# The mixer of a state-space and Fourier diffusion step: order of issue rebuilt per pair (zeros behind the additions, decay factors two pairs ahead, transposes, tables and state matrices one pair later)

## The chip, the core and the metric

The kernel runs on one core of a Trainium2 chip. TensorE multiplies matrices, VectorE and GpSimd do elementwise work, ScalarE does functions and copies, SyncE issues most DMAs. Every engine works through its own queue in order and waits for the others by semaphores. The metric is device time in microseconds of one execution.

## What is computed

Two token sequences (1024 noisy latent tokens, 128 context tokens; 1024 channels) pass two layers. Layer 0 mixes tokens by an S5 state-space recurrence, layer 1 by a Fourier transform; behind each mixer stands a gated ConvFFN, and adaLN columns modulate all of it. Only the S5 mixer is touched here:

```python
abar = jnp.exp(lam * dt)
bbar = ((abar - 1.0) / lam)[..., None] * bmat
bu = jnp.einsum('blgc,gpc->blgp', u, bbar)
bu = bu.at[:, edge].add(abar * h0)
_, h = lax.associative_scan(_linear_recurrence, (a, bu), axis=1, reverse=reverse)
y = jnp.real(jnp.einsum('gcp,blgp->blgc', cmat, h))
```

There are 64 groups of 16 channels with 64 complex states each, in two directions; both sequences go through one pass.

## The kernel before

The mixer takes tokens in frames of eight: KW = 146 columns are 128 frames of the long sequence, two separating columns, and 16 of the short one. What happens inside a frame is a matrix (T, "kernel matrix"); what goes from frame to frame is a scan with the decay of eight steps, in coordinates turned by a phase, so that the scan is real. Groups are worked on in pairs per lane half: a block b is eight groups, four pairs (pr = 0 to 3), and the loop in `run` goes over i = 4b + pr = 0 to 31. All is in float32.

For a pair i:

- `vmm(i)`: TensorE multiplies the frames u by the transposed matrices PT into a PSUM tile V (two buffers), L1503. For i = 2 to 6 it also does a part of the adaLN columns in the same tile (`ada_mm`), finished later by `ada_end`.
- `vin(i)`: ScalarE writes decay factors `dec` (two instructions, L1524) and the columns between the four parts of V (zeros, L1527); VectorE turns V by the phase: B = V sn (L1532), V = V cs (L1533), two additions (L1534, L1535); ScalarE takes the final states (Fin, L1537) and writes one zero column and the initial states h0 (L1538, L1539).
- `scan(i)`: VectorE scans V in place (L1543).
- `vout(i)`: VectorE turns back, into C1 and C2 (L1554 to L1556).
- `wmm(i)`: TensorE adds T times u (L1566) and CA times C (L1572) in one PSUM tile y; ScalarE copies it to `ysb` (L1578).

For a block: `make_p` makes the products P (L1412, L1417, on GpSimd from block 2 on, one buffer) and transposes them on TensorE (`tr[0]`, `tr[1]`: L1425, copied to PT by ScalarE, L1428). `tables` makes cosine and sine: s0 and s1 on VectorE (s0: L1308, L1309; s1: L983, L984), Abs on ScalarE (L1314), four sines and four cosines there (L1322). `make_ca` makes the matrices CA in five GpSimd steps (L1365 to L1370), their `ends` on ScalarE (L1374, L1375), and b-bar (`bb`, L1383 to L1394). `make_t` multiplies Bb by CA (L1447, 64 matmuls in two banks "misc", which the transposes and `make_u` use too), copies the result to kc (L1457 to L1459, ScalarE), adds on GpSimd, and SyncE stores kc to DRAM and loads it back as T. `make_u` normalizes the input of a later block on TensorE and ScalarE (L1475, L1479); `load_u`, `load_x`, `loads` and `store_y` are DMAs on SyncE.

The order of issue is written out by hand: what the loop issues first stands first in each engine's queue. In an iteration come vmm(i + 1), scan(i), vin(i + 1), vout(i), wmm(i - 1), ada_end, and then the block's work for that pr. `pl` is a list of functions called at the end, `late` one called behind it. An instruction on a tile waits for earlier writes of that tile by another engine, as B here waits for the zeros, whose columns it does not read.

Of the kernel before, what the change touches and what calls it, by code (L numbers as in the profile page):

```python
# [16 lines left out]
D = 1024  # L17
# [947 lines left out]
class Ssm:  # L965
# [231 lines left out]
    def squares(self):  # L1197
# [18 lines left out]
        tiles.append(self.sg.tile([128, 1, D], F32, tag="P", bufs=1, name="xt"))  # L1216
# [180 lines left out]
    def make_p(self, b):  # L1397
# [10 lines left out]
        def prod(h, i):  # L1408
            def f():
                if not qs:  # L1410
                    qs.append(self.sg.tile([128, 8, 8], F32, tag="gs", bufs=1, name="gs"))
                    E.tensor_tensor(qs[0], self.G[:, 0, gs], self.G[:, 1, gs], OP.add)  # L1412
                if i == 0:
                    Ps[h] = self.sg.tile([128, 3, 4, 8, 16], F32, tag="P", bufs=1, name="P")
                g = (qs[0], self.G[:, 1, gs], self.G[:, 0, gs])[i]
                hs = slice(4 * h, 4 * h + 4)
                E.tensor_tensor(Ps[h][:, i], g[:, hs, :, None].to_broadcast([128, 4, 8, 16]), x[i][:, hs], OP.mult)  # L1417
            return f
# [96 lines left out]
    def vin(self, i):  # L1515
# [5 lines left out]
        dec = self.sp.tile([128, 2, 2, 148], F32, tag="dec", bufs=2, name="dec")  # L1521
        self.dec[i] = dec
        for dr in range(2):
            nc.scalar.activation(dec[:, :, dr], self.mask[:, None, dr].to_broadcast([128, 2, 148]), AF.Copy,  # L1524
                                 scale=self.r8[:, 2 * i + dr:2 * i + dr + 1])
        f = V.rearrange("p g k -> p (g k)")
        nc.scalar.activation(f[:, V0 + 147:V0 + 147 + 592].rearrange("p (s k) -> p s k", k=148)[:, :, 0:2],  # L1527
                             self.zero[:, None, :].to_broadcast([128, 4, 2]), AF.Copy)
# [9 lines left out]
        nc.scalar.activation(zf[:, :, 130], self.zero, AF.Copy)  # L1538
        nc.scalar.activation(zf[:, :, 0:167:166], self.h0[:, :, 2 * i:2 * i + 2], AF.Copy)  # L1539

# [51 lines left out]
    def run(self):  # L1592
# [47 lines left out]
        call(ca1[1:2])  # L1640
        self.vin(0)
# [6 lines left out]
        nv = 2  # L1648
        for i in range(n + 1):
            b, pr = divmod(i, 4)  # L1650
            n1, n2 = b + 1 < 8, b + 2 < 8
            if nv < n and nv <= i + 1:
                self.vmm(nv)
                nv += 1
# [4 lines left out]
            if i < n:  # L1659
                self.vout(i)  # L1660
            if i:
                self.wmm(i - 1)
# [8 lines left out]
            pl = []  # L1671
            late = [lambda: self.n.early(i - 27)] if i >= 27 else []
            if pr == 0:
# [4 lines left out]
                if n1:  # L1678
                    pp, tr = self.make_p(b + 1)
                    if b:  # L1680
                        tb = self.tables(b + 1)
                        call(tb[:2])
                    call(pp[0])
                    late = tr[0] + tb[2:3]
                if n2 and b:
                    ca, ends, bb = self.make_ca(b + 2)
                    pl = ca[:1] + [lambda: bb[0](self.nc.gpsimd)]
                if not b:
                    pl = ca1[2:] + [ends1]
                    second = Later(self.nc.vector)  # L1690
                    self.phases(second, rest)
                    self.phases16(second, rest)
                    late += [lambda: self.powers(rest, [second])]
            if pr == 1:
                if n1:
                    call(pp[1])
                    late = tb[3:]
                if not b:
                    ca, ends, bb = self.make_ca(2)
                if n2:  # L1700
                    pl = ca[b > 0:3]
                    if b + 3 < 8:
                        self.loads(b + 3)
            if pr == 2:
                if n1:
                    late = tr[1] + [lambda: self.make_t(b + 1)()]
                if n2:
# [3 lines left out]
                    pl = ca[3:4]  # L1711
            if i == 7:
                late = [self.last_frame]
            if pr == 3 and n2:
                self.make_u(b + 2)
                pl = ca[4:] + [ends]
                if b + 3 < 8:
                    self.load_x(b + 3)
            call(pl)
# [157 lines left out]
```

## Time and profile before

| | us |
|---|---|
| median of 3 runs (2499.51 to 2502.55) | 2499.62 |
| profiled execution, its own time | 2499.67 |
| its span, first to last instruction | 2497.9 |
| mixer loop, from the second B (L1532) to the last vout | 70.8 to 381 |
| TensorE busy, share of the span | 93% |
| mean granted TensorE clock | 0.97 |

The loop is an eighth of the run; behind it the kernel is a long row of matmuls, in which TensorE is busy nearly all the time. A timeline row gives start, duration, engine, line and tiles; the brackets tell how long the engine had been idle and which instruction ended that. A granted clock of 1 is TensorE's full speed, 2.4 GHz; 0.5 is 1.2 GHz.

### The profile page before, as it was taken

Reading aid. Unit: us, or ns where it says so; the run is one execution under the profiler, and the core shown is the slowest. Engines: PE = TensorE matmul, PEld = TensorE weight load, DVE = VectorE, ACT = ScalarE, POOL = GpSimd, SP = SyncE. Lnnn points to the kernel's source line nnn. Section 1 sums busy time; section 2 is a strip of 40 time slices with the busy share of each in tenths; the row PEclk is TensorE's granted clock in tenths of the full one; section 3 lists DMA queues with packets and bytes.
Section 4 is the critical chain, followed back from the end, with each engine's and each line's share of the span. In section 5 each row is a group of like instructions: output and inputs, shape, how many; then the busy total and the mean of one; then the engine's idle time right before and its main releaser. Section 6 shows DMA issues by size and latency. Waiting matters only on the chain.

```text
span 2497.9 us, 35759 instructions
## 1 busy us (share of the span) xinstructions
PE 2311.4 (93%) x14754; PEld 2228.0 (89%) x14754; DVE 1499.9 (60%) x2407; ACT 868.4 (35%) x1320; POOL 697.0 (28%) x462
## 2 busy tenths in 40 slices
PE   4668679999999999999999999999999999999996
PEld 3567569787999999999999999989999999999996
DVE  7766766889656454564455473965554555545556
ACT  4444445223523322223222444442232222332234
POOL 6355410226222211222112242622221112211124
PEclk8788799999999999999999999999999999999998
DMA  6323239666111111111111212111111111110112
GB/s 210 101 65 75 59 92 322 220 211 211 35 43 51 44 41 34 35 51 51 35 34 43 68 43 72 60 39 46 44 51 36 33 43 43 51 43 31 38 43 76
DMA packets 94522, 182.33 MB, mean 73 GB/s; under 512 B 16948, under 2 KB 57204, under 8 KB 93336
## 3 DMA queue, kind: packets, MB, share of 16 engines
q1 hardware_dynamic: 90824, 170.67, 21.7%
q0 software_dynamic: 2096, 6.62, 0.8%
q8 instruction: 117, 1.92, 0.3%
q10 hardware_dynamic: 1440, 2.75, 0.3%
q14 instruction: 45, 0.37, 0.0%
HBM read 163.70 MB, written 11.53 MB: 70 GB/s over the span
## 4 chain that ended last, share of the span: by engine, by line
PE 72%; DVE 17%; issue 4%; ACT 3%; DMA 1%; POOL 1%; DVEq 0%; ACTq 0%; POOLq 0%
PE acc L199 62%; DVE c L308 3%; DVE dl L602 2%; DVE dh L602 2%; PE f L839 2%; PE misc L1447 2%; DVE X L916 1%; PE y L1572 1%; DMA w_ada<-w_ada 1%; DVE h L222 1%; PE V L1503 1%; PE f L749 1%; DVE X L363 1%; DVE X L364 1%; PE misc L1425 1%
## 5 line engine op out<-in xcount | busy, mean ns | idle before, releaser
L199 PE MATMUL acc<-h,uh 128*128 128x384 f32 (+1 forms) x4992 | 1015.3, 338 | 1.9 <-DVE d L910 1.3
L199 PEld LDWEIGHTS acc<-h,uh 128*128 128x128 f32 x4992 | 885.2, 188 | 17.7 <-issue 13.2
L183 POOL TENSOR_TENSOR ul<-raw,uh 128x1024 fp32r<-128x1024 f32 x104 | 283.2, 2723 | 1242.2 <-ACT uh L182 1242.2
L199 PE MATMUL acc<-h,ul 128*128 128x384 f32 (+1 forms) x2496 | 571.2, 337 | 0.0
L308 DVE SCALAR_TENSOR_TENSOR c<-t,cw,c 128x896 f32<-128x896 f32 x704 | 347.3, 563 | 202.3 <-ACT c L305 202.3
L199 PEld LDWEIGHTS acc<-h,ul 128*128 128x128 f32 x2496 | 448.2, 189 | 0.0
L182 ACT ACTIVATE uh<-raw 128x1024 fp32r<-128x1024 f32 x108 | 113.6, 1052 | 547.0 <-PE acc L199 501.8
L300 DVE COPY wb<-acc 128x2 f32<-128x2 f32 x88 | 14.0, 159 | 406.1 <-PE acc L199 406.1
L363 DVE SCALAR_TENSOR_TENSOR X<-acc,MOD,X 128x768 f32<-128x768 f32 x168 | 170.1, 1012 | 118.3 <-PE acc L199 118.3
L199 PE MATMUL acc<-gh,dh 128*128 128x384 f32 x960 | 220.8, 337 | 18.4 <-DVE X L365 18.4
L199 PE MATMUL acc<-gl,dh 128*128 128x384 f32 x960 | 218.4, 335 | 0.0
L199 PE MATMUL acc<-gh,dl 128*128 128x384 f32 x960 | 218.2, 334 | 0.0
L199 PEld LDWEIGHTS acc<-gh,dh 128*128 128x128 f32 x960 | 168.8, 188 | 27.1 <-PE acc L199 23.6
L199 PEld LDWEIGHTS acc<-gh,dl 128*128 128x128 f32 x960 | 171.3, 188 | 0.0
L199 PEld LDWEIGHTS acc<-gl,dh 128*128 128x128 f32 x960 | 171.3, 188 | 0.0
L336 ACT ACTIVATE gh<-c 128x1152 fp32r<-128x1152 f32 x44 | 51.4, 1169 | 329.2 <-DVE c L331 290.9
L303 ACT ACTIVATE t<-t,wb 128x1024 f32<-128x1024 f32 x88 | 101.4, 1153 | 152.8 <-DVE t L301 152.8
L183 POOL TENSOR_TENSOR dl<-raw,dh 128x1024 fp32r<-128x1024 f32 x40 | 99.8, 2515 | 165.3 <-ACT dh L182 165.3
L305 ACT ACTIVATE c<-t,cb,cw 128x1152 f32<-128x1152 f32 x88 | 118.9, 1351 | 2.9
L301 DVE TENSOR_TENSOR t<-acc,R 128x1152 f32<-128x1152 f32 x88 | 118.6, 1348 | 0.0
L326 ACT ACTIVATE c<-c 128x1152 f32<-128x1152 f32 x44 | 51.4, 1167 | 152.4 <-DVE c L308 152.3
L1503 PE MATMUL V<-u,PT 128*64 128x146 f32 x512 | 45.7, 328 | 62.0 <-DVE C L1556 61.9
(327 smaller groups left out, 2677.6 us busy)
## 6 DMA issues: line engine op xcount, KB each, us to landing
raw<-w_up SPq DMA_DIRECT2D x88, 512.0 KB, 3.6
w_ada<-w_ada SPq DMA_DIRECT2D x80, 512.0 KB, 5.1
raw<-w_down SPq DMA_DIRECT2D x44, 512.0 KB, 3.6
w_ada<-w_ada SPq DMA_DIRECT2D x8, 1024.0 KB, 5.6
raw<-w_glu SPq DMA_DIRECT2D x16, 512.0 KB, 4.7
u<-hb SPq DMA_DIRECT2D x64, 73.0 KB, 3.3
y_scratch<-ysb SPq DMA_DIRECT2D x8, 584.0 KB, 3.5
xt<-x SPq DMA_DIRECT2D x9, 512.0 KB, 8.8
```

The costliest lines, as they stand in the source:

```text
L182: nc.scalar.activation(hi, raw, AF.Copy)
L183: (E or nc.gpsimd).tensor_tensor(lo, raw, hi.bitcast(F32), OP.subtract)
L199: mm(outs[j], lhsT=w, rhs=r[j], start=first and i == 0, stop=last and i == 2)
L301: nc.vector.tensor_tensor(t.rearrange("p (a b) -> p a b", a=3), p[:, :, :384], self.R.rearrange("p (a b) -> p a b", a=3), OP.mult)
L303: nc.scalar.activation(t[:, :NS], t[:, :NS], AF.Identity, bias=wb[:, 0:1])
L305: nc.scalar.activation(c, t, AF.Identity, bias=cb[:, ui:ui + 1], scale=w(1))
L308: nc.vector.scalar_tensor_tensor(o, a, w(i), o, op0=OP.mult, op1=OP.add)
L326: nc.scalar.activation(c, c, AF.Silu)
L336: nc.scalar.activation(gh, c, AF.Copy)
L363: nc.vector.scalar_tensor_tensor(v, p[:, 0:2, :384], s(0), v, op0=OP.mult, op1=OP.add)
L602: nc.vector.scalar_tensor_tensor(o, i, a, o, op0=OP.mult, op1=OP.add)
L1503: nc.tensor.matmul(V[r, ri, o:o + KW], lhsT=PT[pr // 2][:, ri, 2 * (pr % 2) + dr, r], rhs=x[:, ::-1] if dr else x, start=True, stop=True)
```

## The change

Within vin, the zeros (L1527) are written after the additions, between the zero column and h0. The decay factors become a function of their own: pairs 0 and 1 ahead of the loop, then pair i + 2 behind vout(i). tr[0] goes from pr 0 to pr 1, s1 with Abs, sines and cosines to pr 1 (before: s0, s1, Abs and sines in pr 0, cosines in pr 1); the steps of CA each go about one pair later; make_t is issued ahead of tr[1] in pr 2; make_u and load_x in pr 3 go behind CA's last steps and its ends; P has two buffers. `pl` is now called `fill`, and the products and s0 are called with it. Nothing is computed otherwise.

```diff
--- before.py
+++ after.py
@@ -1213,7 +1213,7 @@
         self.xt = []
         tiles = [sp.tile([128, 1, D], F32, tag=f"PT{i}", bufs=1, name="xt") for i in range(2)]
         tiles += [sp.tile([128, 1, D], F32, tag="ysb", bufs=2, name="xt") for _ in range(2)]
-        tiles.append(self.sg.tile([128, 1, D], F32, tag="P", bufs=1, name="xt"))
+        tiles.append(self.sg.tile([128, 1, D], F32, tag="P", bufs=2, name="xt"))
         tiles += [sp.tile([128, 2, D], F32, tag="CA", bufs=3, name="xt") for _ in range(2)]
         self.xt = [t[:, j] for t in tiles for j in range(t.shape[1])]
         for t, x in enumerate(self.xt):
@@ -1411,7 +1411,7 @@
                     qs.append(self.sg.tile([128, 8, 8], F32, tag="gs", bufs=1, name="gs"))
                     E.tensor_tensor(qs[0], self.G[:, 0, gs], self.G[:, 1, gs], OP.add)
                 if i == 0:
-                    Ps[h] = self.sg.tile([128, 3, 4, 8, 16], F32, tag="P", bufs=1, name="P")
+                    Ps[h] = self.sg.tile([128, 3, 4, 8, 16], F32, tag="P", bufs=2, name="P")
                 g = (qs[0], self.G[:, 1, gs], self.G[:, 0, gs])[i]
                 hs = slice(4 * h, 4 * h + 4)
                 E.tensor_tensor(Ps[h][:, i], g[:, hs, :, None].to_broadcast([128, 4, 8, 16]), x[i][:, hs], OP.mult)
@@ -1518,14 +1518,6 @@
         b, pr = divmod(i, 4)
         cs, sn = self.tab[b]
         V = self.vd[i]
-        dec = self.sp.tile([128, 2, 2, 148], F32, tag="dec", bufs=2, name="dec")
-        self.dec[i] = dec
-        for dr in range(2):
-            nc.scalar.activation(dec[:, :, dr], self.mask[:, None, dr].to_broadcast([128, 2, 148]), AF.Copy,
-                                 scale=self.r8[:, 2 * i + dr:2 * i + dr + 1])
-        f = V.rearrange("p g k -> p (g k)")
-        nc.scalar.activation(f[:, V0 + 147:V0 + 147 + 592].rearrange("p (s k) -> p s k", k=148)[:, :, 0:2],
-                             self.zero[:, None, :].to_broadcast([128, 4, 2]), AF.Copy)
         B = sp.tile([128, 2, 2, KW], F32, tag="B", bufs=1, name="B")
         v = self.view(V).rearrange("p (r d k) -> p r d k", r=2, d=2)[:, :, :, 1:147]
         bc = lambda t: t[:, None, 2 * pr:2 * pr + 2, 1:147].to_broadcast([128, 2, 2, KW])
@@ -1536,7 +1528,16 @@
         zf = self.view(V).rearrange("p (r k) -> p r k", r=2)
         nc.scalar.activation(self.Fin[:, :, 2 * i:2 * i + 2], zf[:, :, 129:166:36], AF.Copy)
         nc.scalar.activation(zf[:, :, 130], self.zero, AF.Copy)
+        f = V.rearrange("p g k -> p (g k)")
+        nc.scalar.activation(f[:, V0 + 147:V0 + 147 + 592].rearrange("p (s k) -> p s k", k=148)[:, :, 0:2],
+                             self.zero[:, None, :].to_broadcast([128, 4, 2]), AF.Copy)
         nc.scalar.activation(zf[:, :, 0:167:166], self.h0[:, :, 2 * i:2 * i + 2], AF.Copy)
+
+    def decay(self, i):
+        dec = self.dec[i] = self.sp.tile([128, 2, 2, 148], F32, tag="dec", bufs=2, name="dec")
+        for dr in range(2):
+            self.nc.scalar.activation(dec[:, :, dr], self.mask[:, None, dr].to_broadcast([128, 2, 148]), AF.Copy,
+                                      scale=self.r8[:, 2 * i + dr:2 * i + dr + 1])
 
     def scan(self, i):
         S = self.view(self.vd[i])
@@ -1638,6 +1639,8 @@
         self.ada_end()
         self.ada_end()
         call(ca1[1:2])
+        self.decay(0)
+        self.decay(1)
         self.vin(0)
         tb = self.tables(1)
         call(tb[:2])
@@ -1645,19 +1648,19 @@
         self.load_u(1)
         self.load_x(2)
         n = 32
-        nv = 2
         for i in range(n + 1):
             b, pr = divmod(i, 4)
             n1, n2 = b + 1 < 8, b + 2 < 8
-            if nv < n and nv <= i + 1:
-                self.vmm(nv)
-                nv += 1
+            if 1 < i + 1 < n:
+                self.vmm(i + 1)
             if i < n:
                 self.scan(i)
             if i + 1 < n:
                 self.vin(i + 1)
             if i < n:
                 self.vout(i)
+            if i + 2 < n:
+                self.decay(i + 2)
             if i:
                 self.wmm(i - 1)
             while self.m_ada:
@@ -1668,8 +1671,7 @@
                 break
             if i == 27:
                 self.made.__exit__(None, None, None)
-            pl = []
-            late = [lambda: self.n.early(i - 27)] if i >= 27 else []
+            fill, late = [], []
             if pr == 0:
                 if n1 and b:
                     self.load_u(b + 1)
@@ -1677,46 +1679,47 @@
                     self.store_y(b - 1)
                 if n1:
                     pp, tr = self.make_p(b + 1)
+                    fill = list(pp[0])
                     if b:
                         tb = self.tables(b + 1)
-                        call(tb[:2])
-                    call(pp[0])
-                    late = tr[0] + tb[2:3]
+                        fill += tb[:1]
                 if n2 and b:
                     ca, ends, bb = self.make_ca(b + 2)
-                    pl = ca[:1] + [lambda: bb[0](self.nc.gpsimd)]
+                    fill.append(lambda: bb[0](self.nc.gpsimd))
                 if not b:
-                    pl = ca1[2:] + [ends1]
+                    fill += ca1[2:] + [ends1]
                     second = Later(self.nc.vector)
                     self.phases(second, rest)
                     self.phases16(second, rest)
-                    late += [lambda: self.powers(rest, [second])]
+                    late = tr[0] + tb[2:3] + [lambda: self.powers(rest, [second])]
             if pr == 1:
                 if n1:
-                    call(pp[1])
-                    late = tb[3:]
+                    fill = list(pp[1])
+                    late = tr[0] + tb[1:] if b else tb[3:]
                 if not b:
                     ca, ends, bb = self.make_ca(2)
                 if n2:
-                    pl = ca[b > 0:3]
+                    fill += ca[:1]
                     if b + 3 < 8:
                         self.loads(b + 3)
             if pr == 2:
                 if n1:
-                    late = tr[1] + [lambda: self.make_t(b + 1)()]
+                    late = [lambda: self.make_t(b + 1)()] + tr[1]
                 if n2:
                     if not b:
                         bb[0]()
                     bb[1]()
-                    pl = ca[3:4]
+                    fill = ca[1:3]
             if i == 7:
                 late = [self.last_frame]
             if pr == 3 and n2:
-                self.make_u(b + 2)
-                pl = ca[4:] + [ends]
+                fill = ca[3:] + [ends]
+                late.append(lambda: self.make_u(b + 2))
                 if b + 3 < 8:
-                    self.load_x(b + 3)
-            call(pl)
+                    late.append(lambda: self.load_x(b + 3))
+            if i >= 27:
+                late.append(lambda: self.n.early(i - 27))
+            call(fill)
             if i == n - 1:
                 self.finals()
             call(late)
```

## Rows read from the trace of the kernel before

**Rows 1.** The head of the page of the profiled execution.

```profile
span 2497.9 us, 35759 instructions
```

**Rows 2.** The waits of VectorE (DVE) from 40 to 385 us: who waited, for whom, us in total, times, longest us.

```profile
DVE B L1532 <- ACT V L1527: 101.6, 31, 11.5
```

**Rows 3.** Busy time in four blocks of the loop (block 1, block 2, a steady block, block 6; block b is the loop's i = 4b to 4b + 3): stretch, its length, busy us of each engine (instructions), granted TensorE clock, DMA share, GB/s.

```profile
121.50:161.50 40.00, 32.81 (x378) 28.72 (x376) 24.51 (x41) 19.54 (x67) 18.21 (x20) 0.91 0.33 81
161.50:203.60 42.10, 28.34 (x310) 24.96 (x308) 29.70 (x41) 17.61 (x58) 21.57 (x21) 0.84 0.22 59
244.50:285.40 40.90, 29.45 (x326) 26.06 (x324) 28.41 (x41) 17.69 (x57) 21.53 (x21) 0.83 0.25 63
326.40:362.90 36.50, 25.23 (x298) 22.24 (x295) 25.66 (x37) 14.68 (x47) 4.43 (x5) 0.86 0.17 49
```

**Rows 4.** The timeline of VectorE in the steady block: start us, duration us, engine, line, operation, tiles, count, and in brackets the idle time before it and what ended that.

```profile
244.49 0.77 DVE L1532 TENSOR_TENSOR B<-V,sn 128x584 f32<-128x584 f32 x1 [2.23 <-ACT V L1527]
...
248.26 1.02 DVE L1308 COPY w<-W 128x144 f32<-128x144 f32 x1
...
251.19 1.36 DVE L983 TENSOR_SCALAR wa<-w 128x896 f32<-128x896 f32 x1
...
252.58 2.69 DVE L984 TENSOR_TENSOR w<-w,wa 128x896 f32<-128x896 f32 x1
...
255.20 1.38 DVE L1543 TENSOR_TENSOR_SCAN V<-dec,V 128x592 f32<-128x592 f32 x1
...
259.66 0.77 DVE L1532 TENSOR_TENSOR B<-V,sn 128x584 f32<-128x584 f32 x1 [3.08 <-ACT V L1527]
...
266.05 0.77 DVE L1532 TENSOR_TENSOR B<-V,sn 128x584 f32<-128x584 f32 x1 [1.23 <-ACT V L1527]
...
278.02 0.77 DVE L1532 TENSOR_TENSOR B<-V,sn 128x584 f32<-128x584 f32 x1 [5.47 <-ACT V L1527]
...
285.40 0.77 DVE L1532 TENSOR_TENSOR B<-V,sn 128x584 f32<-128x584 f32 x1 [2.23 <-ACT V L1527]
```

**Rows 5.** The timeline of ScalarE (ACT) behind the tables of the same block; columns as above.

```profile
255.31 1.07 ACT L1314 ACTIVATE wa<-w 128x1040 f32<-128x1040 f32 x1 [7.35 <-DVE w L984]
...
257.24 1.47 ACT L1322 ACTIVATE sn<-w 128x516 f32<-128x516 f32 x4
...
258.60 0.96 ACT L1524 ACTIVATE dec<-mask,r 128x296 f32<-128x296 f32 x2
...
263.03 1.83 ACT L1322 ACTIVATE cs<-wa,hpi 128x516 f32<-128x516 f32 x4
```

**Rows 6.** The timeline of TensorE (PE), and of the zeros on ScalarE, from the second to the third pair of the same block.

```profile
263.58 2.21 PE L1503 MATMUL V<-u,PT 128*64 128x146 f32 x16 [11.07 <-DVE C L1556]
...
270.00 1.97 PE L1425 MATMUL misc<-ident,P 128*128 128x128 f32 x16
...
271.90 4.61 PE L1447 MATMUL misc<-CA,Bb 64*32 64x128 f32 x64
...
276.44 1.22 PE L1503 MATMUL V<-u,PT 128*64 128x146 f32 x16
...
277.80 0.19 ACT L1527 ACTIVATE V<-zero 128x8 f32<-128x8 f32 x1
...
278.29 2.26 PE L1572 MATMUL y<-C,CA 64*128 64x146 f32 x32
```

**Rows 7.** The timeline of TensorE, ScalarE and SyncE (SPq) in the fourth pair of the same block.

```profile
280.47 2.57 PE L1475 MATMUL misc<-rstd,xb 128*128 128x128 f32 x18
...
281.09 0.40 ACT L1578 ACTIVATE ysb<-y 128x292 f32<-128x292 f32 x1
...
281.39 0.45 ACT L1479 ACTIVATE hb<-misc,b,a 128x128 f32<-128x128 f32 x1
...
282.02 3.64 SPq L1466 DMA_DIRECT2D T<-k_scratch  x8
...
282.98 1.22 PE L1503 MATMUL V<-u,PT 128*64 128x146 f32 x16
...
283.76 0.24 ACT L1374 ACTIVATE CA<-Cm 128x64 f32<-128x64 f32 x1
...
284.35 0.96 ACT L1524 ACTIVATE dec<-mask,r 128x296 f32<-128x296 f32 x2
```

**Rows 8.** The timeline of VectorE in block 1, at the tables, where GpSimd waits.

```profile
125.26 0.23 DVE L1308 COPY w<-W 128x144 f32<-128x144 f32 x1
...
125.40 1.09 DVE L1309 TENSOR_TENSOR w<-W,ph 128x896 f32<-128x896 f32 x1
...
126.53 0.63 DVE L983 TENSOR_SCALAR wa<-w 128x896 f32<-128x896 f32 x1
...
127.19 1.09 DVE L984 TENSOR_TENSOR w<-w,wa 128x896 f32<-128x896 f32 x1
```

**Rows 9.** The timeline ahead of the loop and in its first pair: TensorE, ScalarE, VectorE.

```profile
46.98 1.22 PE L1503 MATMUL V<-u,PT 128*64 128x146 f32 x16
...
57.63 0.97 ACT L1524 ACTIVATE dec<-mask,r 128x296 f32<-128x296 f32 x2
...
58.69 0.77 DVE L1532 TENSOR_TENSOR B<-V,sn 128x584 f32<-128x584 f32 x1 [11.49 <-ACT V L1527]
...
70.75 0.77 DVE L1532 TENSOR_TENSOR B<-V,sn 128x584 f32<-128x584 f32 x1 [4.05 <-ACT V L1527]
```

## The prediction, made before the change was run

> **What bounds the kernel now.** I read the page first, for the span of 2497.9 us [rows 1], then the waits, then the mixer's part of the timeline, because the diff touches nothing behind the mixer loop. All that comes later (gated unit, ConvFFN, Fourier layer) is issued in the same order behind the loop's end, so I take it to move as a block, and time saved in the loop is saved in the run.
>
> Inside the loop the reader is to look for the engine that never gets ahead. In a steady block (244.5 to 285.4 us) VectorE is busy 28.4 of 40.9 us, TensorE 29.5, GpSimd 21.5, ScalarE 17.7 [rows 3]: none is full. VectorE has one kind of wait, 31 times and 101.6 us in all: B (L1532, the first instruction of vin) for ScalarE's zero columns (L1527) [rows 2]. I therefore cut time into steps from one B to the next. From 244.49 they take 15.17, 6.39, 11.97 and 7.38 us, and their waits (in the brackets of the B that ends each) are 3.08, 1.23, 5.47 and 2.23 us [rows 4]: 12.0 of 40.9 us in which VectorE does nothing. Without waits a step has B to the end of vout, 3.77 us (244.49 to 248.26), and the scan, 1.38 us: 5.15 us; on top come whatever fillers sit between.
>
> Behind L1527 stands the rest of ScalarE's queue, in order: after the table step the Abs, PT copies, four sines and the decay factors (255.31 to 259.5) run before the zeros [rows 5]; in the third step six kc copies and the decay factors do [rows 6].
>
> **The change part by part, in a steady block.** I call the iterations 0 to 3 by pr and the step that ends in iteration k's B step k.
>
> *Zeros and decay factors.* Both leave the place ahead of B. Nothing is removed: zeros now cost ScalarE 0.2 us between Fin and h0, and a decay pair 0.9 us [rows 5, 7] behind vout. What B waits for next is TensorE alone (vmm: it starts 3.9 us after the B before, 263.58 against 259.66, and takes 1.22 us [rows 4, 6]). h0 is followed by ysb 3.07 us after B (281.09 against 278.02); with one more write h0 ends near 3.3, and the scan can't start before 3.77. If that cover were gone it would cost 0.2 us a pair, 6 us in all.
>
> *Step 1* (now 15.17). Only the first half of the tables (L1308, L1309) stays on VectorE: 248.26 to 251.19 is 2.93 us [rows 4]. 3.77 + 2.93 + 1.38 = 8.1 us. vmm is long done, the transposes have left this iteration.
>
> *Step 2* (now 6.39). The second half (L983, L984) comes in: 251.19 to 255.20 is 4.0 us [rows 4]. 3.77 + 4.0 + 1.38 = 9.15 us. Beside it TensorE does vmm, wmm (together 4.1 us, 276.44 to 280.55 [rows 6]) and the moved transposes (1.97 us): 6.1 us, hidden. If that cover were gone, 2 us.
>
> *Step 3* (now 11.97). VectorE needs 6.5 us: the present 11.97 less its 5.47 wait, which is 1.35 above 5.15 for the b-bar products (bb) that stay. TensorE starts vmm and wmm 3.9 us after the B before, which is 5.2 us ahead of this one; they end at -1.1 us, the kernel matrix (make_t, 4.54 us, 271.90 to 276.44 [rows 6]) at 3.4. tr[1] (1.97 us) comes behind it now and needs a bank that only the kc copies free, since both share two banks. ScalarE must first finish Abs, sines and cosines (1.07 + 1.47 + 1.83, less 0.1 each for overlap: 4.1 us [rows 5]), which start only when L984 ends. Abs starts 1.3 us before B; 4.1 us later (2.8) comes Fin, the other small writes end at 3.5, the decay pair at 4.4, ysb and the Bb copy (0.3 us each) at 5.05. The first bank is free at 5.6, tr[1] done at 7.6, vmm at 8.85. Step 3 is 8.9 us, with a wait of 2.4.
>
> *Step 0* (now 7.38). VectorE needs 5.15. make_u is now behind the end copies of CA (0.59 us, 283.76 to 284.35 [rows 7]), the decay pair (0.86) and the zeros (0.2). Its third matmul group waits for the first hb copy. Now hb starts 3.37 us after B (281.39 against 278.02); with 1.65 us more ahead, 5.0; hb ends at 5.5, the last group at 6.6, vmm at 7.85. Step 0 is 7.9 us: 0.5 us *slower* than now.
>
> Sum: 8.1 + 9.15 + 8.9 + 7.9 = 34.05 against 40.9 us, 6.85 us a block. Lower bound of the block: VectorE alone, 4 x 5.15 + 1.3 + 2.93 + 4.0 = 28.8. Upper bound: tr[1] 2 us later in step 3 and at the low clock, 37.
>
> *GpSimd and SyncE.* With two P buffers GpSimd no longer waits for the transposes; its 21.5 us a block [rows 3] follow each other from the kc additions on. Counted from iteration 2's B these are done at 6.6, the remaining 21 us at 27.6, and the second half of the tables begins at 8.9 + 7.9 + 8.1 + 3.77 = 28.7. So L983 and L984 may run without GpSimd beside them. Alone they took 0.63 + 1.09 us (126.53, 127.19), against 1.36 + 2.69 beside GpSimd [rows 4, 8]. With 1.7 in place of 4.0 us step 2 falls to 6.85, but TensorE then reaches the kernel matrix later relative to B and step 3 grows to 9.6: 32.45. I keep 4.0, since the margin is 1 us of 27. Here the Trainium skill (SBUF — State Buffer, Who interferes with whom) says that VectorE instructions with two SBUF inputs contend with a GpSimd instruction that reads SBUF, those with one outside the two-port modes do not. The trace agrees: L1532, with one operand in PSUM, lasts 0.77 us everywhere, L984 1.09 or 2.69 [rows 4, 8, 9]. By that rule alone, with the engines apart, the block would be 32.45. SyncE's queue keeps its order (store of kc, loads of T, xb, u, y's store). T's loads are all issued 9 us after the matrix (276.44 to 285.66, which is 282.02 + 3.64 [rows 6, 7]); the new order reads T 15 us after the kc copies, so I price this at nothing. What is left of the cover is 6 us, less their landing; late, it would show as a TensorE wait at L1566.
>
> *Before the loop.* vmm(0) is done at 48.2 (46.98 + 1.22), yet B waits for zeros until 58.69 [rows 9]. Now B, the additions and the tables of block 1 run under ScalarE's work. The two decay pairs (0.86 us each, from 57.63) and the four small writes end near 60.2; scan there, next B at 61.6 in place of 70.75: 9.1 us. Bounds 4 (one wait of 4.05 alone goes) and 11.
>
> *The other blocks.* Block 0 is full on VectorE at its beginning and has ada_mm behind vmm: 2.5 us (bounds 0 and 6). Block 1: 40.0 us now [rows 3], of which the ada columns, which wait for h0, keep some; 4.5 (2 to 7). Block 2: 42.1 - 34.05 = 8.0. Blocks 3 to 5: 3 x 6.85 = 20.5. Block 6 has no CA work, so no GpSimd beside the tables: halves 1.25 and 1.7 us [rows 8], steps 6.4 + 6.9 + 9.5 + 5.3 = 28.1; against 36.5 now [rows 3], and with 0.9 us taken off for the clock, 7.5. Block 7 has neither tables nor transposes: 1.0, an estimate from the 0.2 us of the zeros in four pairs.
>
> Total: 9.1 + 2.5 + 4.5 + 8.0 + 20.5 + 7.5 + 1.0 = 53.1 us. The profiled execution took 2499.67 us, its span 2497.9, so 1.8 us lie around it; the median of the runs is 2499.62, the same to 0.05. 2499.7 - 53.1 gives 2447 us.
>
> **The rivals.**
>
> *Larger gain.* GpSimd is done before L983: 1.6 us less in each of blocks 2 to 5, and prologue and block 1 near their upper bounds: 2499.7 - 63 = 2437. For it: the margin of 1 us. Against: GpSimd instructions themselves stretch when VectorE is beside them.
>
> *TensorE takes the wait.* VectorE's wait for the zeros goes, but vmm stays behind transposes, kernel matrix and make_u. In step 3 now, vmm is done at 277.66 and zeros are written at 277.98 [rows 6]: there TensorE is already as late as ScalarE. If step 3 keeps 12 us, 3 us a block over six blocks, 18 us: 2465. For it: tr[1] waits for kc. Also for it: after 11 us of idling, V ran 2.21 us (263.58) in place of 1.22 (276.44), as at half clock [rows 6]. New gaps might bring that back for 1 to 2 us each: 2.0 us behind tr[0] (done 6.1 us after vmm's start, in a step of 8.1) and 2.3 before tr[1] (3.4 to 5.7).
>
> *Slower: the clock stays low.* TensorE's work in a block is 4 x 4.1 + 2 + 4.6 + 2 + 2.6 = 27.6 us at full clock [rows 6, 7]. At the low level, with V's ratio of 1.8, it is 50 us. It decides from the point where over 60% of that work runs low (27.6 x 1.48 = 40.9). At 50 us in six blocks the time would be 2499.7 + 55 - 12 = 2543. Against it: the granted clock of the steady block is 0.83 with a gap of 11 us in it [rows 3]; the longest in the new order are the two of 2.0 and 2.3 us above.
>
> *The change does not act.* B could still be held by another ScalarE write to the same V. I see none: Fin, zeros and h0 all stand behind the additions now. It would give 2495 to 2500.
>
> **How the numbers follow.** Forecast (savings of 45 to 58 us) 0.52; larger 0.15; TensorE takes the wait (33 to 45 us) 0.25; no effect 0.03; slower 0.05. The likeliest case gives 2447; its own range is 2442 to 2455. Leaving out less than half of the two neighbours at either end gives 2436 to 2466. Within 0.2%, 5 us, this kernel's runs (2499.5 to 2502.6) could not tell a change from none. Faster 0.92, same 0.03, slower 0.05.
>
> **What would show it.** Right: no wait for ScalarE ahead of L1532; waits there only in steps 3 and 0, for vmm, of about 2.4 and 2.7 us; steps near 8.1, 9.2, 8.9, 7.9; V at 1.22 us in all steady pairs and a granted clock above 0.95 from 160 to 310 us; the second B near 61.6. Wrong: a wait of 5 us or more in step 3; V at 2.2 us; L984 at 1.09 (larger gain); a scan that waits for ScalarE's h0, which would mean that the table functions ahead of Fin in iteration 2 are the new bound.

## The result and the profile after

| | before | after |
|---|---|---|
| median of the runs, us | 2499.57 (2498.61 to 2502.55) | 2442.44 (2439.38 to 2443.78) |
| profiled execution, us | 2499.67 | 2443.08 |
| ratio, 95% interval | | 0.9768 (0.9751 to 0.9785) |

The median before now holds a fourth run. The change saves 57 us; 2447 us (2436 to 2466) was forecast. The head of the page after:

```profile
span 2441.3 us, 35730 instructions
```

VectorE's waits from 30 to 330 us (who waited, for whom, us in total, times, longest), against [rows 2]:

```profile
DVE B L1524 <- PE V L1503: 39.9, 12, 4.4
DVE B L1524 <- ACT m_ada L1258: 10.2, 3, 5.9
DVE V L1544 <- ACT V L1534: 6.5, 1, 6.5
```

No B waits for the zeros any more. What is left of more than 2 us in the mixer is TensorE's V, the adaLN columns from block 0 to the start of block 1, and one scan ahead of the loop that waits for h0. The same four blocks as in [rows 3], cut at their B's:

```profile
108.56:142.14 33.58, 28.99 (x361) 25.57 (x359) 24.70 (x41) 19.99 (x67) 18.73 (x20) 0.98 0.29 78
142.14:175.53 33.39, 29.26 (x323) 25.77 (x324) 26.34 (x42) 17.76 (x57) 19.71 (x21) 0.92 0.30 83
209.61:243.71 34.10, 28.40 (x323) 24.98 (x324) 26.98 (x42) 17.75 (x57) 20.36 (x21) 0.95 0.31 85
277.78:305.05 27.27, 24.42 (x305) 21.60 (x306) 22.92 (x37) 14.71 (x47) 1.16 (x3) 1.00 0.25 72
```

VectorE is busy up to 3.4 us less than in [rows 3], the blocks are 6.4 to 9.2 us shorter: most of what went is idle time. The steady block on VectorE, against [rows 4]:

```profile
209.61 0.77 DVE L1524 TENSOR_TENSOR B<-V,sn 128x584 f32<-128x584 f32 x1 [2.72 <-PE V L1503]
...
213.39 1.35 DVE L1308 COPY w<-W 128x144 f32<-128x144 f32 x1
214.66 2.82 DVE L1309 TENSOR_TENSOR w<-W,ph 128x896 f32<-128x896 f32 x1
...
218.71 0.74 DVE L1524 TENSOR_TENSOR B<-V,sn 128x584 f32<-128x584 f32 x1
...
222.45 0.62 DVE L983 TENSOR_SCALAR wa<-w 128x896 f32<-128x896 f32 x1
223.10 1.09 DVE L984 TENSOR_TENSOR w<-w,wa 128x896 f32<-128x896 f32 x1
...
225.41 0.75 DVE L1524 TENSOR_TENSOR B<-V,sn 128x584 f32<-128x584 f32 x1
...
235.82 0.77 DVE L1524 TENSOR_TENSOR B<-V,sn 128x584 f32<-128x584 f32 x1 [3.95 <-PE V L1503]
...
243.71 0.77 DVE L1524 TENSOR_TENSOR B<-V,sn 128x584 f32<-128x584 f32 x1 [2.72 <-PE V L1503]
```

The steps are 9.10, 6.70, 10.41 and 7.89 us, 34.10 in all; 8.1, 9.15, 8.9 and 7.9, 34.05 in all, were forecast. The sum is right to 0.05 us because three errors cancel, and that is luck. Two of them come from GpSimd. From the kc additions on its instructions of a block follow each other almost without a gap, and are called its row here; at the first table half the row is:

```profile
212.72 1.93 POOL L1366 TENSOR_TENSOR CAt<-qs,Cm 128x1024 f32<-128x1024 f32 x1
214.61 1.93 POOL L1367 TENSOR_TENSOR CA<-Qt,Cx 128x1024 f32<-128x1024 f32 x1
216.62 3.09 POOL L1368 TENSOR_TENSOR CA<-CAt,CA 128x1024 f32<-128x1024 f32 x1
```

L1308 ends at 214.74, just behind L1366 (214.65); L1309 then lasts until L1367 is done (216.54) and 0.94 us longer; L1368 takes 3.09 us, where it takes 2.36 with no table instruction beside it. The two engines take turns, one instruction at a time. GpSimd's row ends at 219.71, so the second half, at 222.45, runs alone. The third error is TensorE's:

```profile
222.59 2.21 PE L1503 MATMUL V<-u,PT 128*64 128x146 f32 x16 [3.07 <-DVE C L1557]
...
228.19 4.32 PE L1447 MATMUL misc<-CA,Bb 64*32 64x128 f32 x64
232.69 1.94 PE L1425 MATMUL misc<-ident,P 128*128 128x128 f32 x16 [0.18 <-issue]
234.56 1.22 PE L1503 MATMUL V<-u,PT 128*64 128x146 f32 x16
```

Behind a gap of 3.07 us V runs 2.21 us in place of 1.22, and V and wmm together take 5.6 us (222.59 to 228.19) where 4.1 had been reckoned. The windows of these stretches (columns as in the blocks above) show why:

```profile
213.50:219.60 6.10, 6.00 (x68) 5.26 (x68) 6.10 (x5) 0.65 (x2) 6.02 (x3) 1.00 0.57 170
222.60:228.20 5.60, 5.60 (x53) 4.74 (x53) 5.50 (x8) 5.56 (x13) 0.00 (x0) 0.70 0.02 3
```

The granted clock, 1.00 ahead of the gap, is 0.70 on average behind it: part of this stretch at 1.2 GHz, the rest at 2.4. The kernel matrix begins 2.8 us behind B (225.41), tr[1] and V behind it, and B waits 3.95 us.

Ahead of the loop, on VectorE and ScalarE, against [rows 9]:

```profile
47.54 0.77 DVE L1524 TENSOR_TENSOR B<-V,sn 128x584 f32<-128x584 f32 x1 [0.93 <-PE V L1503]
...
56.84 1.83 ACT L1539 ACTIVATE dec<-mask,r 128x296 f32<-128x296 f32 x4
...
59.39 1.40 DVE L1544 TENSOR_TENSOR_SCAN V<-dec,V 128x592 f32<-128x592 f32 x1 [6.47 <-ACT V L1534]
60.70 0.75 DVE L1524 TENSOR_TENSOR B<-V,sn 128x584 f32<-128x584 f32 x1
```

The first B comes 11.2 us sooner than before; the scan then waits until ScalarE has written the decay factors and h0, a little less long than reckoned (second B 60.70, not 61.6).

### The profile page after: what moved, and what is told of

It reads as the page before. It is cut to its first block, busy times and chain, and to the rows that moved or that the text cites. A ratio compares the mean times of both kernels' runs of the same rounds, so it can differ in the third digit from the quotient of the medians.

```text
span 2441.3 us, 35730 instructions
## 1 busy us (share of the span) xinstructions
PE 2303.3 (94%) x14754; PEld 2223.2 (91%) x14754; DVE 1487.1 (61%) x2407; ACT 870.0 (36%) x1320; POOL 679.7 (28%) x462
## 4 chain that ended last, share of the span: by engine, by line
PE 69%; DVE 16%; issue 6%; POOL 3%; DMA 3%; ACT 2%; SPq 1%; DVEq 0%; ACTq 0%; POOLq 0%
PE acc L199 62%; DVE c L308 3%; DVE dl L602 2%; DVE dh L602 2%; PE f L839 2%; DMA w_ada<-w_ada 1%; DVE X L916 1%; DVE h L222 1%; PE f L749 1%; DVE X L363 1%; DVE X L364 1%; POOL P L1417 1%; PE misc L1447 1%; PE f L199 1%; PE V L1503 1%
## 5 line engine op out<-in xcount | busy, mean ns | idle before, releaser
L183 POOL TENSOR_TENSOR ul<-raw,uh 128x1024 fp32r<-128x1024 f32 x104 | 271.4, 2609 | 1243.3 <-ACT uh L182 1243.3
L602 DVE SCALAR_TENSOR_TENSOR dl<-w_ada,SC,dl 128x1024 f32<-128x1024 f32 x50 | 88.8, 1815 | 0.0
```

What stands on the lines that cost most here:

```text
L183: (E or nc.gpsimd).tensor_tensor(lo, raw, hi.bitcast(F32), OP.subtract)
L602: nc.vector.scalar_tensor_tensor(o, i, a, o, op0=OP.mult, op1=OP.add)
```

## The experiments

Each kernel was timed beside the kernel before (2498.2, 2497.9 or 2497.5 us in its group). First the two halves of the change, each alone.

**The new order alone.** The changed kernel with zeros and decay factors back ahead of B.

```diff
         V = self.vd[i]
+        self.decay(i)
+        f = V.rearrange("p g k -> p (g k)")
+        nc.scalar.activation(f[:, V0 + 147:V0 + 147 + 592].rearrange("p (s k) -> p s k", k=148)[:, :, 0:2],
+                             self.zero[:, None, :].to_broadcast([128, 4, 2]), AF.Copy)
         B = sp.tile([128, 2, 2, KW], F32, tag="B", bufs=1, name="B")
...
-            if i + 2 < n:
-                self.decay(i + 2)
```

> The changed kernel with the zeros and the decay factors put back ahead of B; the new order of the block's work stays. Theory (two gains that overlap: the zeros' move removes waits, the new order removes others): what the zeros' move alone gave is the start, where the second B comes at 60.7 us in place of 70.8, so about 10 us come back; in a steady block ScalarE reaches the zeros only 0.5 us after vmm in step 3 and sooner than vmm elsewhere, so 0 to 1 us a block and 2 to 3 us in the two blocks with adaLN columns: 2453 to 2460 us, a steady block of 34 to 35 us. Rival (the zeros' wait of 101.6 us was the whole cause, the order is nothing): the waits for the zeros come back in full and the time is 2485 us or more, a steady block 40 us.

2473.95 us (ratio 0.9900, 0.9886 to 0.9915), between the two expectations. VectorE in a steady block (L1528 is B here, L1523 the zeros):

```profile
205.19 0.74 DVE L1528 TENSOR_TENSOR B<-V,sn 128x584 f32<-128x584 f32 x1
215.84 0.77 DVE L1528 TENSOR_TENSOR B<-V,sn 128x584 f32<-128x584 f32 x1 [3.85 <-ACT V L1523]
227.25 0.77 DVE L1528 TENSOR_TENSOR B<-V,sn 128x584 f32<-128x584 f32 x1 [4.92 <-ACT V L1523]
```

I had overlooked that in the new order PT copies, Abs, sines and cosines stand ahead of the zeros in step 2: a wait of 3.85 us. Step 3 waits 4.92 us for them here. The order alone gives 24 us.

**The zeros alone.** The kernel before with zeros and decay factors moved as the change moves them, all else as it was.

```diff
         nc.scalar.activation(zf[:, :, 130], self.zero, AF.Copy)
+        nc.scalar.activation(f[:, V0 + 147:V0 + 147 + 592].rearrange("p (s k) -> p s k", k=148)[:, :, 0:2],
+                             self.zero[:, None, :].to_broadcast([128, 4, 2]), AF.Copy)
...
                 self.vout(i)
+            if i + 2 < n:
+                self.decay(i + 2)
```

> The kernel before with the zeros behind the additions and the decay factors two pairs ahead; everything else in the old order, one P buffer. Theory: step 1 loses its 3.1 us wait (15.2 to 12.1); steps 2 and 3 together stay at 18.3 us, because TensorE, which starts after 11 us of idling at the low clock, does vmm, wmm, tr[1], the kernel matrix and the next vmm in one row (3.9 + 6.45 + 2.1 + 4.5 + 1.3); step 0 stays at 7.3. A steady block of 37.7 us, 3.2 less than before, so 19 us over six blocks and 12 at the start: 2466 to 2474 us. Rival (the zeros are the whole): 2443 to 2450 us, a steady block of 34 to 35 us.

2452.87 us (0.9816, 0.9801 to 0.9830): 45 us, much more than expected and nearer the rival. Its steady block, 34.0 us, is as short as that of the full change (steps of 9.5, 5.5 to 6.2, 11.4 to 11.8 and 7.3). Tables in pr 0 should have cost 6.9 us; VectorE's and GpSimd's rows there show why they cost 4.4:

```profile
217.41 1.08 DVE L1309 TENSOR_TENSOR w<-W,ph 128x896 f32<-128x896 f32 x1
218.53 1.36 DVE L983 TENSOR_SCALAR wa<-w 128x896 f32<-128x896 f32 x1
219.93 1.83 DVE L984 TENSOR_TENSOR w<-w,wa 128x896 f32<-128x896 f32 x1
...
218.31 1.10 POOL L1417 TENSOR_TENSOR P<-gs,Bb 128x512 f32<-128x512 f32 x1 [2.13 <-PE misc L1425]
```

With one P buffer GpSimd stands idle for 2.13 us, waiting for the transposes, just as the tables start. The rebuilt order earns its further 10 us (2452.87 against 2442.44) elsewhere: block 6 takes 32.3 us here and 27.3 in the changed kernel, block 1 35.3 and 33.6; the rest is smaller.

**A second P buffer in that kernel** tests this reading.

```diff
-    self.sg.tile([128, 3, 4, 8, 16], F32, tag="P", bufs=1, name="P")
+    self.sg.tile([128, 3, 4, 8, 16], F32, tag="P", bufs=2, name="P")
```

> The kernel before with the zeros and the decay factors moved (2452.9 us, steady block 34.0), and P with two buffers as the only further edit. There the tables in pr 0 cost 4.4 us since GpSimd, with one P buffer, stood for 2.1 us waiting for the transposes just as they ran. Theory, taking turns: with two buffers the row goes on, and each of the four table instructions waits for the rest of a product or a CA step: L1309 about 1.95, L983 2.3 or more, L984 2.7 or more, 7 to 9 us together in place of 4.4. TensorE's gap behind them grows by as much, and V behind it is slower. Steady block 37 to 40, 2464 to 2478: a second buffer makes this order slower. Rival, the tables were cheap for another reason: block 34, 2449 to 2455.

2468.11 us (0.9881, 0.9866 to 0.9896), steady block 38. GpSimd no longer stands idle, and every table instruction waits for it (8.3 us together):

```profile
190.33 1.05 DVE L1308 COPY w<-W 128x144 f32<-128x144 f32 x1
191.30 1.95 DVE L1309 TENSOR_TENSOR w<-W,ph 128x896 f32<-128x896 f32 x1
193.29 2.24 DVE L983 TENSOR_SCALAR wa<-w 128x896 f32<-128x896 f32 x1
195.56 3.11 DVE L984 TENSOR_TENSOR w<-w,wa 128x896 f32<-128x896 f32 x1
```

The buffer that removes GpSimd's wait costs this order 15 us.

**One P buffer in the changed kernel** (the same edit, the other way).

> The changed kernel with one P buffer. Theory (what the two table halves cost is set by whether GpSimd runs beside them): GpSimd then waits for tr[0] before it can make the second products, so the first half runs alone (1.25 in place of 3.95 us) and the second beside GpSimd (4.0 in place of 1.65); TensorE's 3-us gap behind tr[0] goes as well. Step 1 about 6.4, step 2 about 9.1, step 3 about 9, step 0 7.9: a steady block of 32.3 in place of 34.1 us, 2432 to 2438 us. Rival (the second buffer is part of the gain): GpSimd's wait makes P or CA late, TensorE or ScalarE wait for it, and the time is 2446 us or more.

2450.04 us (0.9811, 0.9797 to 0.9826): the rival's time, but not by its mechanism. The first table half is alone as I had expected (L1309 1.08). But GpSimd's row now comes later and meets the b-bar products in step 3, and the copy of Bb, ahead of the kc copies on ScalarE, waits for them:

```profile
234.35 1.28 DVE L1383 TENSOR_TENSOR Bb<-Bm,beta 128x128 f32<-128x128 f32 x1
235.87 2.31 DVE L1385 TENSOR_TENSOR Bb<-Bb,Bx 128x128 f32<-128x128 f32 x1
...
238.27 0.42 ACT L1394 ACTIVATE Bb<-Bb 128x256 f32<-128x256 f32 x1 [2.81 <-DVE Bb L1385]
```

Alone these products take 0.28 to 0.29 us each. Step 3 takes 13.1 us or more.

**Smaller instructions.** The changed kernel with CA's GpSimd instructions halved, the sharpest test of taking turns.

```diff
+        def halves(o, x, y, op):
+            for s in (slice(0, 4), slice(4, 8)) if b > 1 else (slice(0, 8),):
+                E.tensor_tensor(o[:, s], x[:, s], y[:, s], op)
...
-        st = [first, lambda: E.tensor_tensor(re, bcq(1), bcc(cx[:, 0]), OP.mult),
+        st = [first, lambda: halves(re, bcq(1), bcc(cx[:, 0]), OP.mult),
```

> The changed kernel with each of the five GpSimd instructions of CA (1024 columns, 1.93 and 2.36 us) split into two of 512 columns from block 2 on; nothing else. GpSimd does the same work and some 1 us more of it. Theory, taking turns: what a table instruction waits for is the rest of one GpSimd instruction, now at most 1.2 us. L1308 about 0.9 (now 1.35), L1309 about 1.9 to 2.0 (now 2.82), step 1 7.7 to 8.1 in place of 9.10; TensorE's gap ahead of V is shorter by as much, so V may be back at 1.22 us and step 3 up to 1 us shorter. Block 31.8 to 33.0, 2433 to 2439. Rival, both engines are slowed while they overlap, whatever the size of an instruction: L1309 stays at 2.5 to 2.9, step 1 at 8.9 to 9.4, 2440 to 2446.

2434.64 us (0.9748, 0.9732 to 0.9764), as expected; steps 7.5, 6.7, 8.84, 7.88, a block of 30.9 us, are even shorter, but block 1 gives back 3.6 us (37.15 against 33.58), which was not followed up. VectorE and GpSimd (x2 are two instructions in a row):

```profile
211.53 0.64 DVE L1308 COPY w<-W 128x144 f32<-128x144 f32 x1
212.09 1.95 DVE L1309 TENSOR_TENSOR w<-W,ph 128x896 f32<-128x896 f32 x1
...
211.02 2.07 POOL L1364 TENSOR_TENSOR CAt<-qs,Cm 128x512 f32<-128x512 f32 x2
```

L1309 waits for one instruction of half the size, 1.95 us in place of 2.82. TensorE's gap is 1.48 us instead of 3.07, the granted clock behind it 1.00, V takes 1.22 us, step 3 is 1.6 us shorter. GpSimd has 0.7 us more to do in a block (2.07 for 1.93 three times, 2.51 for 2.36 twice), and the kernel is 8 us faster. Had the engines only slowed each other while they overlap, as the rival has it, L1309 would have stayed at 2.5 us or more.

**The tables back together in pr 0, in the changed kernel.**

```diff
-                        fill += tb[:1]
+                        fill += tb[:2]
...
-                    late = tr[0] + tb[1:] if b else tb[3:]
+                    late = tr[0] + tb[2:] if b else tb[3:]
```

> The changed kernel with the second half of the tables on VectorE (L983, L984) put back into pr 0, directly behind the first half; Abs, sines and cosines stay in pr 1. Theory: both halves then run beside GpSimd, so the second half takes 4.0 us in place of 1.65, and step 1 grows by 4 us to 13.1, while steps 2 and 3 together stay, being TensorE's row from vout on (17.1 us): 4 us in each of blocks 2 to 5, 3 in block 1, 1.7 in block 6: 2458 to 2466 us, steady block 38 us. Rival (splitting is neutral, the two halves cost the same wherever they stand): step 1 longer by 1.65 and step 2 shorter by 1.65, 2440 to 2445 us.

2468.98 us (0.9878, 0.9862 to 0.9895), steady block 38 with a step 1 of 12.9 (L983 2.67 in place of 0.62). The theory holds, and the price is 3 us above its range: splitting the tables is worth 26.5 us here.

**tr[1] ahead of the kernel matrix again.**

```diff
-    late = [lambda: self.make_t(b + 1)()] + tr[1]
+    late = tr[1] + [lambda: self.make_t(b + 1)()]
```

> The changed kernel with tr[1] ahead of the kernel matrix in pr 2, as before the change. Theory: ScalarE, busy with sines and cosines, evicts the transposes only about 2.3 us after TensorE has made them, the kernel matrix needs both banks and starts late, vmm behind it too: step 3 grows from 10.4 to about 12.1 us, 1.7 us a block: 2449 to 2456 us. Rival (TensorE has the same work in either order): 2440 to 2445 us, step 3 at 10.4.

2460.14 us (0.9846, 0.9832 to 0.9861): direction as expected, more than the size. The matrix waits 3.9 us for the PT copies behind the sines and cosines and then runs 5.9 to 7.3 us in blocks 2 to 5 in place of 4.32, at a granted clock of 0.59 in block 4 (240.4 to 247.5 us); B waits 6.3 to 7.7 us. The expectation had not counted on the clock.

**The kernel matrix in pr 0.**

```diff
                         fill += tb[:1]
+                        late = [lambda: self.make_t(b + 1)()]
...
-                    late = [lambda: self.make_t(b + 1)()] + tr[1]
+                    late = tr[1] if b else [lambda: self.make_t(b + 1)()] + tr[1]
```

> The changed kernel with the kernel matrix of the next block made in pr 0 instead of pr 2 (blocks from 1 on). Theory (step 3 is long because TensorE does vmm, wmm, the kernel matrix and tr[1] in one row): the 4.5 us move to where TensorE idled, step 3 falls from 10.4 to 6.5 us, all VectorE's; step 1 becomes TensorE's with 8.6; the second table half meets GpSimd, which had to wait for kc, and takes 4.0, so step 2 rises to 9.1: 32.2 us a block in place of 34.1, 2427 to 2435 us. Rival (ScalarE's functions behind L984 hold step 3): step 3 stays over 9 us and the time is 2441 us or more.

2456.76 us (0.9833, 0.9818 to 0.9847), 14 us slower than the changed kernel where 7 to 15 faster had been expected. The time and a step 3 over 9 us are the rival's, but not by its mechanism: the wait in step 3 went. GpSimd's row hangs on the kc copies. It now starts in pr 0 and falls on the second table half (L983 1.89, L984 2.70) and on the b-bar products (L1383 1.73); step 0 waits 4.6 us for V behind tr[1]. Steps 9.1, 9.6, 9.1, 9.8.

**make_u ahead of CA's ends and the decay pair.**

```diff
-            if i + 2 < n:
+            if i + 2 < n and not (pr == 3 and n2):
...
-                fill = ca[3:] + [ends]
+                fill = ca[3:]
                 late.append(lambda: self.make_u(b + 2))
+                late.append(ends)
+                late.append(lambda: self.decay(i + 2))
```

> The changed kernel with make_u ahead of CA's end copies and of the decay factors in pr 3. Theory (step 0 is set by the first hb copy, which stands behind end copies and decay on ScalarE, with TensorE waiting): hb starts 1.45 us sooner, step 0 falls from 7.9 to 6.45 us in blocks 0 to 5: 8 us, 2432 to 2437 us. Rival (TensorE's own row of wmm and make_u sets it): step 0 stays above 7.4 and the time within 3 us of 2442.

2421.19 us (0.9699, 0.9685 to 0.9714), better than expected. Step 0 is 6.44, as reckoned. The rest is phase, that is, where GpSimd's row stands in time against VectorE's instructions: steps 1 and 3 fell to 6.57 and 8.79 as well, while step 2 rose from 6.70 to 7.72. The row's end has moved against VectorE:

```profile
202.91 0.45 DVE L1308 COPY w<-W 128x144 f32<-128x144 f32 x1
203.28 1.21 DVE L1309 TENSOR_TENSOR w<-W,ph 128x896 f32<-128x896 f32 x1
...
209.46 1.64 DVE L983 TENSOR_SCALAR wa<-w 128x896 f32<-128x896 f32 x1
```

L1308 and L1309 now meet the end of a product and an instruction of 0.32 us, L983 the last CA step of the row. Every V of the steady blocks is at 1.22 us.

**Both halves of the tables in pr 1.**

```diff
-                        fill += tb[:1]
...
-                    late = tr[0] + tb[1:] if b else tb[3:]
+                    late = tr[0] + tb if b else tb[3:]
```

> The changed kernel with both halves of the tables in pr 1. Theory (contention with GpSimd): the first half then starts about when GpSimd ends its row, and costs 1.2 to 2.2 us in place of 3.95; step 1 falls to 5.2, steps 2 and 3 together come to 17.9, step 0 stays at 7.9: 31 us a block in place of 34.1, 2421 to 2431 us. Rival (the halves cost the same anywhere): 4 us move from step 1 to step 2, TensorE's row starts sooner by as much, and the block is 33 to 34 us, 2436 to 2442.

2426.18 us (0.9716, 0.9700 to 0.9732), as expected: steps 5.2, 8.2, 8.8 and 7.9 us, a block of 30.1; the tables meet only the end of GpSimd's row (L1308 0.45).

**Both of these at once,** with the two diffs just shown.

> Two changes at once that were measured one by one: make_u ahead of CA's ends and the decay factors in pr 3 (2421.2 us), and both halves of the tables in pr 1 (2426.2). Theory, taking turns: VectorE's table instructions wait until the GpSimd instruction under way ends and then run their own duration. In the steady block GpSimd's row ends 17.2 us behind iteration 2's B in the run with the tables in pr 1 (211.32 against 194.13). Here steps 0 and 1 are 6.4 and 5.2 us, so the tables start 6.4 + 5.2 + 3.8 = 15.4 us behind that B and meet the last GpSimd instruction of the row: L1308 about 1.9 in place of 0.2 to 0.45 us, the others alone. Step 2 grows from 8.2 to 9.7 or 9.9, the block is 30.0 to 30.4: nothing won against either, 2421 to 2428. Rival, the gains add: steps 5.2, 8.2, 8.8, 6.4, block 28.6, 2410 to 2417.

2423.85 us (0.9707, 0.9692 to 0.9721): the gains don't add. One detail differs: not every block is 30.2 us, blocks of 31.7 and 28.5 alternate. L1308 in one block and in the next, with the GpSimd instruction ahead of each:

```profile
208.81 1.90 DVE L1308 COPY w<-W 128x144 f32<-128x144 f32 x1
...
240.47 0.31 DVE L1308 COPY w<-W 128x144 f32<-128x144 f32 x1
...
208.25 2.37 POOL L1368 TENSOR_TENSOR CA<-CAt,CA 128x1024 f32<-128x1024 f32 x1
...
238.32 2.37 POOL L1368 TENSOR_TENSOR CA<-CAt,CA 128x1024 f32<-128x1024 f32 x1
```

A block that meets the row's end is long: its step 3 is 10.4 us in place of 8.8. The tables of the next start 15.4 us behind the B that ends it, as before, but the row now ends 15.6 us behind that B in place of 17.2, almost in time.

**make_u first, and the decay pair behind the kernel matrix too.**

```diff
-            if i + 2 < n and not (pr == 3 and n2):
+            if i + 2 < n and not (pr > 1 and n2):
...
                     late = [lambda: self.make_t(b + 1)()] + tr[1]
+                    if n2:
+                        late.append(lambda: self.decay(i + 2))
```

> make_u ahead of CA's ends and the decay factors in pr 3 (2421.2 us, block 29.5), and in pr 2 the decay factors behind the kernel matrix and tr[1] too. In the steady block of that run the decay pair (217.04 to 217.91) stands ahead of the kc copies on ScalarE, whose bank tr[1] waits for after the matrix (gap of 1.15 us ahead of 219.09). Theory, ScalarE's queue sets step 3: kc copies 0.9 us sooner, step 3 7.9 to 8.1 in place of 8.79 (wait 1.4 to 1.6 in place of 2.33), the rest as it was: block 28.6 to 28.8, 2414 to 2419. Rival, the gap is TensorE's own and nothing of ScalarE's: step 3 stays 8.8, 2420 to 2427.

2419.71 us (0.9686, 0.9672 to 0.9701), the lowest median, but no longer distinct from 2421.19. Step 3 fell by 0.1 us, not 0.8. ScalarE is free sooner, and then waits for VectorE's b-bar product, as this row of it shows:

```profile
217.73 0.42 ACT L1394 ACTIVATE Bb<-Bb 128x256 f32<-128x256 f32 x1 [0.65 <-DVE Bb L1385]
```

The rival's step 3, and its time to within 0.3 us, but by a third cause: the copy of Bb, ahead of the kc copies, starts 4.65 us behind B, where it was 4.76. The next link of the chain lay 0.1 us behind the one removed.

## Why the prediction came out right

*The mechanism* (zeros held B) is settled: B's waits for them are gone, and moving them alone gives 45 of the 57 us. The rivals "the change does not act" and "the clock stays low" are out (granted clock 0.92 to 1.00 in the four blocks, 0.83 to 0.91 in [rows 3]).

*The sum, term by term,* in us, measured from B to B:

| term | reckoned | measured |
|---|---|---|
| before the loop (second B 70.75 to 60.70) | 9.1 | 10.0 |
| block 0 (50.74 to 47.86) | 2.5 | 2.9 |
| block 1 (40.04 to 33.58) | 4.5 | 6.5 |
| block 2 (42.08 to 33.39) | 8.0 | 8.7 |
| blocks 3 to 5 | 20.5 | 20.5 |
| block 6 (36.54 to 27.27) | 7.5 | 9.3 |
| block 7 | 1.0 | 1.0 |

This makes 58.8 against 53.1; 1.7 us of it is lost behind the loop by the medians and 2.2 by the two spans, no more than the spread of the runs. Block 6 was sized too low by the 0.9 us that I took off for the clock (it is at 1.00) and 0.9 in its steps. Block 1 was taken near its middle; it came out near its upper bound of 7.

*The steps that failed.* Both table halves were priced by durations copied from [rows 4], 2.93 and 4.0 us; they took 4.0 and 1.7. Such a duration is no property of the instruction: it holds what was left of the GpSimd instruction under way. I did see that the row might end before L983, and it did, yet I kept the contended price and left the first half out of that question, where a CA step of 1.93 us had come to stand. Step 3 was reckoned with ScalarE's chain as the bound, tr[1] at 5.6 us behind B; the kernel matrix ended at 7.1, since step 2 was 2.45 us shorter and TensorE ran its V and wmm 1.5 us slower. The prediction's own figure for that case (step 2 6.85, step 3 9.6, together 16.45) came within 0.7 us of the 17.11 measured, though it had no slow stretch in it. The claim that V stays at 1.22 us in all steady pairs was wrong in one of four.

*The rivals.* The larger gain's mechanism came true (L984 at 1.09), but a shorter step 2 handed most of it to step 3. TensorE's wait in step 3 is 3.95, not 2.4, but far from step 3 keeping its 12 us; the sign of half clock that spoke for it did show. So two of the prediction's own signs of being wrong, V at 2.2 us and L984 at 1.09, came with a time inside its range: the mechanism of the gain held, the working of steps 1 to 3 did not. Step 0 was right to 0.1 us, make_u's delay included, and that delay was worth far more than its own 1.4 us when undone.

*Open.* Why the order rebuild and the zeros' move overlap by about 12 us (24 and 45 alone, 57 together) is followed only through the steady block, block 1 and block 6. Zeros and decay factors were only ever moved together, so what each gives is not known apart. Of the 58.8 us, 58.2 are still there at 1490 us of the trace before, and 1.6 go between there and 1611 us, far behind the loop; why is not known, nor whether the alternation of blocks would last over more of them.

## What to carry to other kernels

Before a wait is priced, write down what stands ahead of the writer in its own queue, and move an unrelated small write behind the work that nobody waits for. When work is moved against an engine that shares something with another, price each instruction by what will be running beside it then, not by its duration in the old trace; and try the cheap knobs of phase, such as smaller instructions, since gains of moves that act through phase need not add.

## What was not expected of the hardware

*VectorE and GpSimd take turns by the instruction.* In the traces of both kernels and the twelve others a table instruction (L1308, L1309, L983, L984) that finds a GpSimd instruction at work lasts for the rest of that one and its own duration alone (0.22, 1.08, 0.62, 1.09 us) less 0.13, and never less than its own. Of the 448 table instructions in these traces 196 began beside one, and the rule gives 195 of their durations within 0.02 us; in the other the two began within 0.01 us of each other, and VectorE did not wait. The 252 others took their duration alone. It holds the other way too: L1368 above, held until L1309's end at 217.48, would by the rule take 0.86 + 2.36 - 0.13 = 3.09 us, and did. The Trainium skill (SBUF — State Buffer, Who interferes with whom) says that whoever issues first keeps the shared ports for the whole instruction and the other blocks; the traces agree, to the 0.02 us above, for COPY, TENSOR_SCALAR and TENSOR_TENSOR alike. B, with an operand in PSUM, stays at 0.74 to 0.77 us in all of them.

*TensorE behind a gap.* V took 1.22 us behind gaps of 1.07 us (make_u first) and 1.48 (halved CA), 2.21 behind 3.07 (the changed kernel) and 2.22 behind 8.46 (zeros alone with two P buffers). Behind 4.61 us it took 1.52 to 2.22 in five blocks of one kernel (zeros alone). V alone misleads there: where it lost less, wmm behind it lost more, as in the steady block of that run, where wmm's two parts take 0.77 and 2.26 at full clock:

```profile
226.86 1.67 PE L1503 MATMUL V<-u,PT 128*64 128x146 f32 x16 [4.61 <-DVE C L1557]
228.45 1.34 PE L1567 MATMUL y<-u,T 128*128 128x146 f32 x4
229.72 2.81 PE L1573 MATMUL y<-C,CA 64*128 64x146 f32 x32
```

The granted clock is 1.00 in V's first 0.6 us (226.86 to 227.46) and 0.50 behind them (227.50 to 230.00). V and wmm together last 5.6 us here and 5.6 behind 3.07 us in the changed kernel, 4.0 where the clock is 1.00. I had priced gaps of 2 us at 1 to 2 us each as a risk; here 3 us cost 1.0 in V and 0.5 in wmm, and 1.5 cost nothing.
